# Moving the split weights of a transformer block by 64 bytes in SBUF

## The chip, the core and the metric

The kernel runs as one program on one core of a Trainium2 chip. The metric is the device time of one execution in microseconds (us). Times before: 2294.86 us, the median of three runs (2291.57 to 2296.39).

## What is computed

One transformer block on x, 512 tokens by 2048 features, in float32:

```python
h    = rms_norm(x, norm_mix_pre)
proj = h @ w_in                      # 2048 x 6680: attention q, six k/v sets, gates, retention q, k, v, g
o_a  = nsa_attention(...)            # 8 heads: compressed, selected and window branch, gated
o_r  = silu(g_r) * retention(rope(q_r), rope(k_r), v_r, log_gamma)
x    = x + rms_norm(concatenate([o_a, o_r]) @ w_out, norm_mix_post)
h    = rms_norm(x, norm_mlp_pre)
u    = square(relu(h @ w_up))        # 2048 x 8192
x    = x + rms_norm(u @ w_down, norm_mlp_post)
```

## The kernel before

**Three products for one.** Every large float32 product is made of three matmuls in the type float32r. An operand is split into a high part, which ScalarE makes by casting, and a low part, which VectorE makes by subtracting the high part from the source (`split`, lines 142 to 144; in the feed-forward half lines 948 and 926). `mm3` (lines 153 to 156) then issues high by high, high by low and low by high into one PSUM bank. Of the two operands of a matmul the stationary one (its first) is 128 columns that are loaded into the array by a weight load, the moving one streams past it. Each matmul has a weight load of its own; the names below are in the order moving, stationary, as the profile prints them.

**The operands.** `Hh` and `Hl` hold the split activations (16 slices of 512 columns each). `whi` and `wlo` hold the split weights, in slabs that are fetched from HBM, split and then used. Which is moving and which stationary depends on the stage:

- *Projection w_in.* The first block of it (`v0`) takes its slabs from a pool `early`, 280 columns wide. All others take them from the pool `wp`, slabs of two slices of 512 columns with three buffers. In `feat_major` the activations move (512 columns) and the weights are stationary: `mm<-Hh,whi`. In `tok_major` the weights move (512 columns, in one block 256) and the activations are stationary: `mm<-whi,Hh`. Between these products a second stream of work, the attention and retention units, is issued at fixed points (class `Side`).
- *Output projection w_out.* `tok_major` with the pool `wp`, 416 columns, four blocks; then a last block of 384 columns from a pool `res`.
- *Up projection.* The product with w_up is done by a scheme with seven half-size products per block (`ORDER`), 256 columns of activations moving (`Hh`, `Hl`, or their sums `sx`), the weights stationary: `prod<-Hh,whi`, `prod<-sx,whi`. The slabs come from the pool `hilo` (three buffers of `whi`, three of `wlo`), filled by the class `Feed`, which runs up to three slabs ahead: fetch into `low` or `Y`, sum where the scheme wants one, cast, subtract.
- *Down projection.* The same seven products, with the weights moving (512 columns) and the hidden activations, which now lie in `Hh` and `Hl`, stationary: `prod<-whi,Hh`.

**Where they lie.** A partition of SBUF is one row of bytes. Tile pools on the left side are stacked upward from a fixed start; pools opened with `side="right"` are stacked downward from the top, which in the built program is byte 229344. An unused tile in a pool of its own (`gap_h`, `gap_w`, `gap_r`) therefore only shifts what is stacked after it. On the left `misc` comes first, and `Hh` starts at byte 17056, `Hl` at 49824: both are 160 modulo 256. All their slices are multiples of 512 bytes, so every operand taken from them starts at 160 modulo 256. On the right, in the first half of the kernel, the raw slabs (`wr`, 3 x 4096 bytes) come first, then `gap_w` with 128 bytes, then `wp` (6 x 4096 bytes), which so starts at 192352, or 96 modulo 256; below it lie the tiles of the retention units. In the second half all these have been released, and `hilo` (6 x 4096 bytes) starts at 204768, or 224 modulo 256, with `low` below it. The sums `sx` lie at 160, the slabs of `res` at 64. A slab in `early` has 2240 bytes, which is 192 more than a multiple of 256, so its eight slabs start at four different places.

With the place of the moving operand minus that of the stationary one, modulo 256 and as a signed number, the large products before are:

| products | moving, stationary | columns | matmuls | difference, bytes |
|---|---|---|---|---|
| w_in, `feat_major` | Hh/Hl, whi/wlo in `wp` | 512 | 1536 | +64 |
| w_in, `tok_major` | whi/wlo in `wp`, Hh/Hl | 512 | 768 | -64 |
| w_in, `tok_major` | whi/wlo in `wp`, Hh/Hl | 256 | 192 | -64 |
| w_in, `v0` | whi/wlo in `early`, Hh/Hl | 280 | 192 | eight values |
| w_out | whi/wlo in `wp`, Hh/Hl | 416 | 768 | -64 |
| w_out, last block | whi/wlo in `res`, Hh/Hl | 384 | 192 | -96 |
| up | Hh/Hl/sx, whi/wlo in `hilo` | 256 | 5376 | -64 |
| down | whi/wlo in `hilo`, Hh/Hl | 512 | 2688 | +64 |

The lines that decide this are:

```python
    gw = wctx.enter_context(tc.tile_pool(name="gapw", bufs=1, side="right"))
    gw.tile([P, 32], F32, name="gap_w")
    wp = wctx.enter_context(tc.tile_pool(name="wp", bufs=3, side="right"))
    ...
    hp = ctx.enter_context(tc.tile_pool(name="hilo", bufs=3, side="right", reuse_waits="tile"))
    rw = ctx.enter_context(tc.tile_pool(name="raws", bufs=1, side="right", reuse_waits="tile"))
```

Of the kernel before, what the change touches and what calls it, by code (L numbers as in the profile page):

```python
# [10 lines left out]
F32 = mybir.dt.float32  # L11
# [5 lines left out]
P = 128  # L17
# [95 lines left out]
def block_kernel(ctx: ExitStack, tc: tile.TileContext, x, norm_mix_pre, w_in, cmp_pe_k, cmp_w1_k, cmp_b1_k,  # L113
# [149 lines left out]
    side = Side()  # L263
# [33 lines left out]


    gw = wctx.enter_context(tc.tile_pool(name="gapw", bufs=1, side="right"))
    gw.tile([P, 32], F32, name="gap_w")  # L300
    wp = wctx.enter_context(tc.tile_pool(name="wp", bufs=3, side="right"))
    pool_a = lambda: (wp, S)
    actx, rctx = ExitStack(), ExitStack()
# [560 lines left out]

    ptp = ctx.enter_context(tc.tile_pool(name="ptp", bufs=2, space=PS, side="right"))
    pr0 = ctx.enter_context(tc.tile_pool(name="pr0", bufs=1, space=PS, side="right"))
    hp = ctx.enter_context(tc.tile_pool(name="hilo", bufs=3, side="right", reuse_waits="tile"))
    rw = ctx.enter_context(tc.tile_pool(name="raws", bufs=1, side="right", reuse_waits="tile"))
    low = rw.tile([P, 6144], F32, name="low")
# [518 lines left out]
```

## Time and profile before

| | |
|---|---|
| median of the runs | 2294.86 us |
| the profiled execution | 2292.01 us |
| its span, first to last instruction | 2290.2 us |
| TensorE matmul busy | 2193.3 us (96% of the span), 12787 matmuls |
| weight loads busy | 1923.0 us (84%) |
| VectorE busy | 1563.9 us (68%) |
| ScalarE busy | 986.9 us (43%) |
| mean granted TensorE clock | 0.986 |

A matmul's own duration in the profile includes the time that its first column needs to reach the end of the array, and successive matmuls overlap. So the time that a matmul takes from the engine is read from the start of one to the start of the next, in the view that lists instructions in order of time, or from the number of matmuls in a stretch in which the engine never waits.

### The profile page before, as it was taken

The numbers are of one execution on the slowest core, as the hardware profiler recorded it, in microseconds if no ns is written. First come the engines' busy times: TensorE is split into PE (matmuls) and PEld (weight loads), VectorE is DVE, ScalarE is ACT, GpSimd is POOL, SyncE is SP. The second block draws the span as 40 slices with busy tenths as digits, with TensorE's granted clock in tenths as the row PEclk, the third lists the DMA queues.
The fourth block names the chain that finished last, engine by engine and source line by source line (L and its number), as shares of the span: only waits on it lengthen the run. The fifth ranks groups of instructions, "written<-read, shape, count | busy, mean of one in ns | idle before, by whom it ended". The sixth has DMA issues, their size and how long they took to land.

```text
span 2290.2 us, 31776 instructions
## 1 busy us (share of the span) xinstructions
PE 2193.3 (96%) x12787; PEld 1923.0 (84%) x12787; DVE 1563.9 (68%) x1868; ACT 986.9 (43%) x1432; POOL 122.1 (5%) x133
## 2 busy tenths in 40 slices
PE   8799999999999999989999999999899999999994
PEld 7578878878787899879899999999777888888873
DVE  6122556554655533487788888888768998899897
ACT  5022344243232323464455555555554444444442
POOL 0000000000000000000000000000000000000002
PEclk9899999999999999989999999999999999999997
DMA  6552322322223334557867676767565656566555
GB/s 190 88 154 88 111 69 88 97 74 79 82 82 119 105 105 133 181 177 203 217 193 197 180 196 178 196 179 208 174 227 165 203 160 202 153 200 176 180 151 83
DMA packets 251622, 346.02 MB, mean 151 GB/s; under 512 B 14315, under 2 KB 163131, under 8 KB 250833
## 3 DMA queue, kind: packets, MB, share of 16 engines
q1 hardware_dynamic: 210960, 287.18, 38.9%
q0 software_dynamic: 30416, 45.25, 12.6%
q10 hardware_dynamic: 10098, 11.55, 1.5%
q8 instruction: 100, 1.64, 0.3%
q14 instruction: 48, 0.39, 0.0%
HBM read 299.90 MB, written 44.04 MB: 150 GB/s over the span
## 4 chain that ended last, share of the span: by engine, by line
PE 75%; DVE 11%; DMA 6%; ACT 3%; issue 3%; POOL 1%; SPq 0%; POOLq 0%; ACTq 0%; DVEq 0%
PE prod L155 13%; PE prod L156 13%; PE prod L154 13%; PE mm L154 10%; PE mm L156 10%; PE mm L155 10%; DVE wlo L926 3%; DMA raw<-in_w_in 3%; DMA low<-in_w_up 2%; DVE Hl L144 2%; PE S L580 2%; ACT whi L948 1%; DVE Y L944 1%; DVE low L944 1%; DVE acc L1284 1%
## 5 line engine op out<-in xcount | busy, mean ns | idle before, releaser
L948 ACT CAST whi<-low 128x1024 fp32r<-128x1024 f32 x234 | 245.3, 1052 | 306.4 <-DVE low L944 116.0
L155 PE MATMUL prod<-wlo,Hh 128*128 128x512 f32 x896 | 354.6, 396 | 15.6 <-DVE wlo L926 15.1
L144 DVE TENSOR_TENSOR wlo<-raw,whi 128x1024 fp32r<-128x1024 f32 (+4 forms) x152 | 168.5, 1113 | 283.5 <-ACT whi L143 272.2
L156 PE MATMUL prod<-whi,Hl 128*128 128x512 f32 x896 | 352.2, 393 | 0.0
L154 PE MATMUL prod<-whi,Hh 128*128 128x512 f32 x896 | 350.7, 391 | 0.0
L948 ACT CAST whi<-Y 128x1024 fp32r<-128x1024 f32 x214 | 223.9, 1049 | 287.8 <-DVE Y L944 107.2
L926 DVE TENSOR_TENSOR wlo<-low,whi 128x1024 fp32r<-128x1024 f32 x234 | 285.1, 1222 | 63.1 <-ACT whi L948 61.4
L156 PE MATMUL prod<-Hh,wlo 128*128 128x256 f32 x1024 | 286.6, 280 | 12.7 <-DVE wlo L926 12.7
L926 DVE TENSOR_TENSOR wlo<-Y,whi 128x1024 fp32r<-128x1024 f32 x214 | 260.6, 1222 | 53.6 <-ACT whi L948 52.1
L143 ACT CAST whi<-raw 128x1024 fp32r<-128x1024 f32 (+4 forms) x152 | 145.5, 959 | 333.4 <-PE mm L155 127.3
L154 PE MATMUL prod<-Hh,whi 128*128 128x256 f32 x1024 | 286.3, 280 | 2.9 <-DVE Y L821 2.3
L155 PE MATMUL prod<-Hl,whi 128*128 128x256 f32 x1024 | 285.4, 279 | 0.0
L154 PE MATMUL mm<-whi,Hh 128*128 128x416 f32 (+4 forms) x704 | 263.7, 375 | 0.8 <-ACT Hh L143 0.8
L156 PE MATMUL mm<-whi,Hl 128*128 128x416 f32 (+4 forms) x704 | 249.2, 354 | 0.7 <-DVE Hl L144 0.7
L155 PE MATMUL mm<-wlo,Hh 128*128 128x416 f32 (+4 forms) x704 | 248.9, 354 | 0.0
L154 PE MATMUL mm<-Hh,whi 128*128 128x512 f32 x512 | 218.6, 427 | 15.0 <-ACT whi L143 9.5
L155 PEld LDWEIGHTS prod<-wlo,Hh 128*128 128x128 f32 x896 | 168.5, 188 | 64.8 <-DVE wlo L926 28.1
L156 PE MATMUL prod<-sx,wlo 128*128 128x256 f32 x768 | 214.0, 279 | 6.5 <-DVE wlo L926 6.5
L154 PE MATMUL prod<-sx,whi 128*128 128x256 f32 x768 | 213.7, 278 | 0.8 <-ACT whi L948 0.8
L155 PE MATMUL prod<-sx,whi 128*128 128x256 f32 x768 | 213.5, 278 | 0.0
L156 PEld LDWEIGHTS prod<-Hh,wlo 128*128 128x128 f32 x1024 | 194.5, 190 | 14.5 <-DVE wlo L926 14.4
L156 PE MATMUL mm<-Hh,wlo 128*128 128x512 f32 x512 | 204.2, 399 | 0.1
(259 smaller groups left out, 3953.8 us busy)
## 6 DMA issues: line engine op xcount, KB each, us to landing
raw<-in_w_in SPq DMA_DIRECT2D x160, 256.0 KB, 3.1
low<-in_w_up SPq DMA_DIRECT2D x39, 1024.0 KB, 6.0
Y<-in_w_up SPq DMA_DIRECT2D x33, 1024.0 KB, 6.0
Y<-in_w_down SPq DMA_DIRECT2D x32, 1024.0 KB, 5.3
low<-in_w_down SPq DMA_DIRECT2D x32, 1024.0 KB, 5.2
Y<-ud SPq DMA_DIRECT2D x49, 512.0 KB, 9.0
ud<-Y SPq DMA_DIRECT2D x72, 256.0 KB, 4.7
raw<-in_w_out SPq DMA_DIRECT2D x32, 416.0 KB, 3.4
```

The costliest lines, as they stand in the source:

```text
L143: nc.scalar.copy(hi, src)
L144: nc.vector.tensor_sub(lo, src, hi.bitcast(F32))
L154: nc.tensor.matmul(ps, ah, bh, start=first, stop=False)
L155: nc.tensor.matmul(ps, ah, bl, start=False, stop=False)
L156: nc.tensor.matmul(ps, al, bh, start=False, stop=last)
L580: nc.tensor.matmul(sps[:, :c + L], QT[g][:, h, qs], k, start=True, stop=True)
L926: nc.vector.tensor_sub(lo, src, hi.bitcast(F32))
L944: nc.vector.tensor_add(to, to, by)
L948: nc.scalar.copy(hi, src)
L1284: nc.vector.tensor_add(e[p], ps, e[p])
```

## The change

`gap_w` is made 64 bytes instead of 128, so that everything stacked after it on the right (`wp` and the retention tiles) lies 64 bytes higher: `wp` starts at 192416, or 160 modulo 256. In front of `hilo` a new unused tile of 64 bytes, `gap_m`, is stacked, so that `hilo` and `low` lie 64 bytes lower: `hilo` starts at 204704, or 160 modulo 256. No instruction is added, removed or reordered. The difference of the table becomes 0 in every row except that of `v0` and that of the last block of w_out, which stay as they are.

```diff
     gw = wctx.enter_context(tc.tile_pool(name="gapw", bufs=1, side="right"))
-    gw.tile([P, 32], F32, name="gap_w")
+    gw.tile([P, 16], F32, name="gap_w")
     wp = wctx.enter_context(tc.tile_pool(name="wp", bufs=3, side="right"))
...
     pr0 = ctx.enter_context(tc.tile_pool(name="pr0", bufs=1, space=PS, side="right"))
+    gh = ctx.enter_context(tc.tile_pool(name="gaph", bufs=1, side="right"))
+    gh.tile([P, 16], F32, name="gap_m")
     hp = ctx.enter_context(tc.tile_pool(name="hilo", bufs=3, side="right", reuse_waits="tile"))
```

## Rows read from the trace of the kernel before

**Rows 1.** Busy time by stretch: us, then PE, PEld, DVE, ACT, POOL, PEclk, DMA share, GB/s

```profile
130.00:967.00 837.00, 833.32 (x4181) 709.46 (x4180) 409.39 (x736) 277.55 (x576) 18.06 (x32) 1.00 0.34 100
967.00:1143.00 176.00, 153.32 (x1218) 149.37 (x1218) 138.12 (x147) 93.66 (x123) 12.78 (x11) 0.95 0.71 201
1143.00:1620.00 477.00, 475.69 (x4194) 475.49 (x4195) 387.25 (x388) 266.25 (x327) 30.57 (x24) 1.00 0.68 190
1620.00:2250.00 630.00, 616.08 (x2655) 496.85 (x2655) 556.53 (x484) 302.74 (x313) 37.86 (x32) 1.00 0.60 178
```

**Rows 2.** Waits from 1143 to 1613 us: us in total, times, longest

```profile
ACT whi L948 <- PE prod L155: 136.5, 123, 1.7
...
PEld prod L156 <- DVE wlo L926: 0.7, 1, 0.7
```

**Rows 3.** Matmuls in order of time, w_in `feat_major`: start us, us, what

```profile
559.85 0.40 PE L154 MATMUL mm<-Hh,whi 128*128 128x512 f32 x1
...
578.87 0.39 PE L156 MATMUL mm<-Hh,wlo 128*128 128x512 f32 x1
```

**Rows 4.** Matmuls in order of time, down projection

```profile
1959.66 0.39 PE L155 MATMUL prod<-wlo,Hh 128*128 128x512 f32 x1
...
1979.11 0.39 PE L156 MATMUL prod<-whi,Hl 128*128 128x512 f32 x1
```

**Rows 5.** Matmuls in order of time, w_in `tok_major`, 512 columns

```profile
731.24 0.39 PE L154 MATMUL mm<-whi,Hh 128*128 128x512 f32 x1
...
750.61 0.39 PE L156 MATMUL mm<-whi,Hl 128*128 128x512 f32 x1
```

**Rows 6.** Busy time in stretches of one product: 416, 384, 256, 256 and 512 columns

```profile
812.00:928.00 116.00, 116.00 (x623) 116.00 (x622) 38.78 (x45) 35.02 (x59) 1.61 (x3) 1.00 0.38 114
930.00:950.00 20.00, 20.00 (x117) 20.00 (x117) 7.23 (x15) 6.98 (x16) 1.65 (x3) 1.00 0.69 216
1030.00:1065.00 35.00, 35.00 (x300) 35.00 (x299) 26.93 (x26) 17.53 (x22) 3.90 (x3) 1.00 0.69 174
1145.00:1610.00 465.00, 465.00 (x4105) 465.00 (x4105) 377.96 (x378) 259.21 (x318) 30.57 (x24) 1.00 0.68 189
1878.00:1926.00 48.00, 48.00 (x211) 39.41 (x210) 41.63 (x36) 19.05 (x19) 2.36 (x2) 1.00 0.56 154
```

**Rows 7.** Busy time and granted clock just after a wait, 256 columns

```profile
972.20:975.00 2.80, 2.80 (x15) 2.80 (x15) 1.69 (x2) 2.19 (x3) 0.00 (x0) 0.50 0.00 0
```

**Rows 8.** Matmuls in order of time in that stretch

```profile
973.06 0.41 PE L155 MATMUL prod<-Hl,whi 128*128 128x256 f32 x1
...
974.98 0.41 PE L155 MATMUL prod<-Hl,whi 128*128 128x256 f32 x1
```

**Rows 9.** Matmuls in order of time, `v0`, last two slabs, 280 columns

```profile
47.86 0.29 PE L154 MATMUL mm<-whi,Hh 128*128 128x280 f32 x1
...
48.25 0.29 PE L154 MATMUL mm<-whi,Hh 128*128 128x280 f32 x1
...
48.63 0.29 PE L154 MATMUL mm<-whi,Hh 128*128 128x280 f32 x1
...
49.02 0.29 PE L154 MATMUL mm<-whi,Hh 128*128 128x280 f32 x1
...
49.41 0.39 PE L154 MATMUL mm<-Hh,whi 128*128 128x512 f32 x1
```

**Rows 10.** Costliest groups on the page: casts and subtractions from two sources

```profile
L948 ACT CAST whi<-low 128x1024 fp32r<-128x1024 f32 x234 | 245.3, 1052 | 306.4 <-DVE low L944 116.0
L948 ACT CAST whi<-Y 128x1024 fp32r<-128x1024 f32 x214 | 223.9, 1049 | 287.8 <-DVE Y L944 107.2
L926 DVE TENSOR_TENSOR wlo<-low,whi 128x1024 fp32r<-128x1024 f32 x234 | 285.1, 1222 | 63.1 <-ACT whi L948 61.4
L926 DVE TENSOR_TENSOR wlo<-Y,whi 128x1024 fp32r<-128x1024 f32 x214 | 260.6, 1222 | 53.6 <-ACT whi L948 52.1
```

## The prediction, made before the changed kernel had run

> **What bounds the kernel now.** I read the busy shares first, then busy time by stretch, then the waits, and last the matmuls one by one. TensorE is busy for 96% of the span. By stretch it has almost no idle time once the start is over: 833.3 of 837 us in the projections and the attention, 475.7 of 477 in the up projection, 616.1 of 630 in the down projection; only in the change from the first half to the second (967 to 1143 us) does it lose 23 us, at a mean granted clock of 0.95 [rows 1]. VectorE is busy for 88% of the down projection (556.5 of 630) and less elsewhere. In the up projection TensorE's longest-waited releaser is worth 0.7 us in 470, while ScalarE waits 136.5 us for TensorE to give slab buffers back [rows 2]: the feed is ahead, the matmuls set the pace. So the time is the number of matmuls times the spacing of their starts, and nothing is in front of TensorE to hide a change of that spacing.
>
> **The spacing is larger than the columns ask for, and not everywhere by the same.** The reader divides the time between two rows by the matmuls between them (the count is mine, from the full list of the stretch).
>
> - 512 columns, moving operand 64 bytes above the stationary one (modulo 256): 83 intervals from 559.85 to 578.87 us, 229.2 ns each [rows 3]; in the down projection 85 intervals from 1959.66 to 1979.11, 228.8 ns [rows 4]. I take 229.0.
> - 512 columns, moving operand 64 bytes below: 83 intervals from 731.24 to 750.61, 233.4 ns [rows 5].
> - 416 columns, 64 below: 116 us hold 623 rows, of which two began before or are cut off, so 186.8 ns; 384 columns, 96 below: 20 us for 115, 173.9 ns [rows 6].
> - 256 columns, 64 below: 465 us for 4103 matmuls, 113.3 ns, without a single wait; but from 1030 to 1065 us the same kind of matmul at the same places took 35 us for 298, 117.4 ns [rows 6]. So there are at least two steady rhythms for one placement.
>
> All of these ran at a granted clock of 1.00, the 2.4 GHz level, at which a column takes 0.417 ns: 512 columns 213.3 ns, 416 173.3, 384 160.0, 256 106.7. The surplus is 15.7, 20.1, 13.5, 13.9 and 6.6 (or 10.7) ns. In a stretch with a granted clock of 0.50, the 1.2 GHz level [rows 7], which followed a wait, 9 intervals from 973.06 to 974.98 us give 213.3 ns for 256 columns [rows 8]: exactly the columns, no surplus. So the surplus belongs to the fast clock, when operands are read twice as fast, and between the two placements of 512 columns it differs by 4.4 ns. Roles don't explain that: in rows 4 and 5 alike weights move past `Hh` and `Hl`, and only the places differ.
>
> *What the skill says against it.* The Trainium skill, "TensorE: Matmul & The Clock Gate", Part 2, "Step-by-step: what each phase is for", says that the streaming operand and the weight load have independent read ports in SBUF, so that the next weight load takes no bandwidth from the running matmul; by that rule the place of one against the other changes nothing and the sum is 0. Rows 4 and 5 differ all the same, so the trace does not fully agree; the rule's result is the second rival below.
>
> **The change part by part.** Nothing is added on any queue; three things move.
>
> *The weights in `wp` and `hilo`: the difference becomes 0 in all products but `v0` and the last block of w_out.* The trace of before shows the difference 0 in one place only, the first half of the last slab of `v0`, 280 columns: three matmuls from 48.63 to 49.02 us, 130 ns each. Its neighbours at -64, +32 and +96 bytes took 130, 127 and 130 ns (47.86 to 48.25, to 48.63; 49.02 to 49.41) [rows 9]. That rules out that the surplus goes away at difference 0 (280 columns alone are 116.7 ns), and it shows no penalty, but three matmuls are too few to settle into a rhythm. So I bound 512 columns at difference 0 by the long rows: below by 226.7 ns, which is 213.3 plus the 13.4 that 384 and 416 columns pay, above by the 233.4 of rows 5. Difference 0 lies as far from +64 as from -64, so I take the middle of their rows, 231.2 ns. With 1536 + 2688 = 4224 matmuls now at 229.0 and 768 at 233.4, that is 4224 x 2.2 = +9.3 us and 768 x -2.2 = -1.7 us, together +7.6 us. For 256, 384 and 416 columns there is no second placement in a long row; nearest are their own rows, so I leave 113.3 and 186.8 as they are, with 117.4 as the dear end of 256 (4103 matmuls x 4.1 = +16.8 us) and the bare columns as the cheap end (4103 x -6.6 = -27.1 us, and 768 x -13.5 = -10.4 us for 416).
>
> *Other readers and writers of the moved tiles.* The cast of a slab takes 1052 ns from `low` (224 modulo 256) and 1049 ns from `Y` (32 modulo 256), the subtraction 1222 ns from both [rows 10]. So the place does not matter to ScalarE and VectorE by more than 3 ns in 1050, some 2 us over all slabs, and that lies beside TensorE: cost 0.
>
> *The transfers into `low` and into the raw slabs that borrow buffers of `wp`.* They land 64 bytes lower or higher, at the same place modulo 64. If they took longer, the cover is the feed's lead: ScalarE waits 136.5 us for free buffers [rows 2], against 448 casts in all, so a landing could be late by some 0.3 us each before it reached TensorE. I take 0.
>
> The sum against the profiled execution: 2292.0 + 7.6 = 2299.6 us. Its time lies 2.9 us under the median of the runs, so for the median I say 2302.5 us. All of it passes through, since TensorE does not wait where the matmuls are; were 512 columns cheaper instead, VectorE, busy 41.6 of 48 us in the down projection [rows 6], would follow down to 87% of today's time.
>
> **Rivals.**
>
> 1. *The dearer rhythm everywhere.* At difference 0 both streams begin in the same 256-byte place and hinder one another as in the worst rows seen: 512 columns at 233.4 (4224 x 4.4 = +18.6 us) and 256 at 117.4 (+16.8 us): +35.4, 2330 us. For it: the second rhythm exists already, and an operand that trails by 64 costs more than one that leads. Against it: the row at difference 0 is no dearer than its neighbours [rows 9].
> 2. *No dependence on the difference.* Either nothing changes, or only the place of the moving operand itself counts: at 160 and 224 (rows 3 and 4) it costs 229, at 96 (rows 5) 233.4, and after the change all lie at 160, so -4.4 x 768 = -3.4 us. 2291.5 to 2295 us, no change. For it: rows 9, where eight placements cost the same. Against it: rows 3 to 5 fit a difference as well.
> 3. *The other side: faster, because streams in the same place hinder each other once and then run in step.* Then 512 columns would pay what 384 and 416 pay, 226.7 ns: 4224 x -2.3 = -9.7 and 768 x -6.7 = -5.1 us: 2280 us. It decides from 228.5 ns downward for 512 columns, if 256 columns stay. For it: the surplus of 512 columns varies with the place, and that of 416 is smaller with more than two thirds of its columns. Against it: the 280 columns at difference 0 still pay 13.3 ns.
> 4. *The surplus goes away.* 512 columns at 213.3, 256 at 106.7, 416 at 173.3: 66 + 15 + 37 + 10 = -128 us, 2167 us. Against it: rows 9.
>
> That the change does not do what it says is no rival here: the two tiles shift the stack, and the places follow from sizes.
>
> **How the numbers follow.** The forecast, 512 columns between 229.0 and 233.4 and the rest unchanged, gets 0.30; its own range is 2294 to 2314 us, and 0.05 of the 0.30 lies within 0.2% (4.6 us, about what runs of this kernel can tell from no change). Rival 1 gets 0.18, rival 2 0.25 (0.02 of it faster and 0.01 slower by more than 0.2%), rival 3 0.22 (0.01 within), rival 4 0.05. Slower: 0.25 + 0.18 + 0.01 = 0.44. Same: 0.05 + 0.22 + 0.01 = 0.28. Faster: 0.02 + 0.21 + 0.05 = 0.28. The range from 2275 to 2334 us holds the forecast and rivals 1 to 3 with little beyond their prices; rival 4 and the far ends of the others are left out.
>
> **What would show it.** In the profile of the changed kernel: the spacing of 512-column starts in the same three places (229 to 233 ns: forecast; 226.7 or less: rival 3; 229 in all three: rival 2); the number of 256-column matmuls per stretch of the up projection (113.3 ns: forecast; 117.4 or more: rival 1; towards 106.7: rival 4); 416 columns at 186.8 ns; casts and subtractions at 1050 and 1222 ns. The prediction is wrong in kind if the 256-column spacing moves, for I have set it to stay and it has the most matmuls; it is wrong in its base if idle time of TensorE changes by more than a few microseconds where it now waits for nothing.

## The result, and the profile after

The changed kernel takes 2316.73 us (median of 10 runs, 2314.88 to 2318.20), against 2296.05 us for the kernel before on the same chip (median of 10, 2291.57 to 2312.66): 1.0076 times as long, 95% interval 1.0051 to 1.0100. It is slower, by 20.7 us between the medians. One execution of the kernel before in the experiments below took 3644.9 us, at a mean granted clock of 0.557, and counts in no comparison. The profiled execution took 2316.6 us, 24.6 us more than the profiled one of before.

The stretches of the changed kernel, cut at the same points of the work as [rows 1] (us, then PE, PEld, DVE, ACT, POOL, PEclk, DMA share, GB/s):

```profile
130.00:964.00 834.00, 830.50 (x4178) 710.32 (x4177) 408.33 (x734) 276.50 (x572) 18.02 (x32) 1.00 0.34 100
964.00:1145.00 181.00, 160.29 (x1237) 156.59 (x1236) 142.47 (x151) 96.34 (x128) 12.77 (x11) 0.95 0.71 201
1145.00:1648.00 503.00, 502.13 (x4182) 501.93 (x4182) 384.51 (x385) 265.42 (x324) 30.57 (x24) 1.00 0.64 179
1648.00:2275.00 627.00, 611.78 (x2657) 496.88 (x2656) 556.61 (x484) 302.65 (x313) 37.84 (x32) 1.00 0.60 178
```

The reader is to see where the time went. The up projection, the third row, became longer by 26 us with nearly the same number of matmuls (4182 after 4194) and, as before, hardly any idle time of TensorE. The change from the first half to the second became 5 us longer, the projections and the down projection 3 us shorter each. So the spacing of the matmuls changed, in both directions. The same stretches of one product as in [rows 6], in the changed kernel (416, 384, 256, 256 and 512 columns):

```profile
808.00:926.00 118.00, 118.00 (x628) 117.32 (x627) 39.08 (x46) 35.17 (x59) 1.61 (x3) 1.00 0.38 115
930.00:948.00 18.00, 18.00 (x106) 18.00 (x105) 5.83 (x13) 6.54 (x15) 1.20 (x3) 1.00 0.65 208
1030.00:1062.00 32.00, 32.00 (x269) 32.00 (x268) 23.68 (x24) 14.77 (x19) 3.44 (x3) 1.00 0.66 166
1147.00:1640.00 493.00, 493.00 (x4110) 493.00 (x4109) 378.44 (x379) 259.23 (x317) 30.57 (x24) 1.00 0.64 178
1905.00:1950.00 45.00, 45.00 (x200) 37.27 (x199) 39.02 (x34) 17.93 (x18) 2.36 (x2) 1.00 0.59 163
```

With the two records that belong to the edges taken off, 4108 matmuls of 256 columns in 493 us are 120.0 ns each, against 113.3 [rows 6]; the earlier stretch, 267 in 32 us, has 119.9 against 117.4. The 512-column products are read from starts in order of time, three pairs of first and last row: `feat_major` as [rows 3], 82 intervals, `tok_major` as [rows 5], 82, and the down projection as [rows 4], 87:

```profile
558.92 0.39 PE L154 MATMUL mm<-Hh,whi 128*128 128x512 f32 x1
...
577.50 0.39 PE L155 MATMUL mm<-Hl,whi 128*128 128x512 f32 x1
...
729.23 0.39 PE L154 MATMUL mm<-whi,Hh 128*128 128x512 f32 x1
...
747.81 0.39 PE L155 MATMUL mm<-wlo,Hh 128*128 128x512 f32 x1
...
1981.16 0.40 PE L156 MATMUL prod<-whi,Hl 128*128 128x512 f32 x1
...
2000.90 0.39 PE L156 MATMUL prod<-whi,Hl 128*128 128x512 f32 x1
```

They give 226.6, 226.6 and 226.9 ns, where there were 229.2, 233.4 and 228.8. All three products with both operands in the same place, modulo 256 bytes, run alike, whichever operand moves, and all are cheaper than before.

Casts and subtractions did not change, as on the page of the changed kernel (its line numbers are 2 higher there; before: [rows 10]):

```profile
L950 ACT CAST whi<-low 128x1024 fp32r<-128x1024 f32 x234 | 244.9, 1050 | 321.2 <-PE prod L155 107.8
L928 DVE TENSOR_TENSOR wlo<-low,whi 128x1024 fp32r<-128x1024 f32 x234 | 285.0, 1222 | 71.4 <-ACT whi L950 70.0
```

Summing start to start over all matmuls of a product, waits included, accounts for the difference between the two profiled executions: up projection 675.3 us against 645.6 (+29.7), down projection 636.9 against 640.3 (-3.4), 512 columns of w_in 582.5 against 586.4 (-3.9), its 256 columns 23.8 against 23.0 (+0.8), 416 columns 145.0 against 143.9 (+1.1); together +24.3 of the 24.6 us.

### The profile page after: what moved, and what is told of

Same layout as the page of the kernel before. It is cut to its first block, busy times and chain, and to the rows that moved or that the text cites. A ratio compares the mean times of both kernels' runs of the same rounds, so it can differ in the third digit from the quotient of the medians.

```text
span 2314.8 us, 31776 instructions
## 1 busy us (share of the span) xinstructions
PE 2218.8 (96%) x12787; PEld 1957.2 (85%) x12787; DVE 1564.1 (68%) x1868; ACT 987.7 (43%) x1432; POOL 122.0 (5%) x133
## 4 chain that ended last, share of the span: by engine, by line
PE 76%; DVE 11%; DMA 6%; ACT 3%; issue 3%; POOL 1%; SPq 0%; POOLq 0%; ACTq 0%; DVEq 0%
PE prod L155 14%; PE prod L156 13%; PE prod L154 13%; PE mm L154 10%; PE mm L156 10%; PE mm L155 10%; DVE wlo L928 3%; DMA raw<-in_w_in 3%; DMA low<-in_w_up 2%; DVE Hl L144 2%; PE S L580 2%; ACT whi L950 1%; DVE Y L946 1%; DVE low L946 1%; DVE acc L1286 1%
## 5 line engine op out<-in xcount | busy, mean ns | idle before, releaser
L950 ACT CAST whi<-low 128x1024 fp32r<-128x1024 f32 x234 | 244.9, 1050 | 321.2 <-PE prod L155 107.8
L928 DVE TENSOR_TENSOR wlo<-low,whi 128x1024 fp32r<-128x1024 f32 x234 | 285.0, 1222 | 71.4 <-ACT whi L950 70.0
L156 PE MATMUL prod<-Hh,wlo 128*128 128x256 f32 x1024 | 293.0, 286 | 9.5 <-DVE wlo L928 9.4
L928 DVE TENSOR_TENSOR wlo<-Y,whi 128x1024 fp32r<-128x1024 f32 x214 | 260.6, 1222 | 58.5 <-ACT whi L950 57.1
L154 PE MATMUL prod<-Hh,whi 128*128 128x256 f32 x1024 | 292.9, 286 | 2.3 <-DVE Y L821 2.3
L155 PE MATMUL prod<-Hl,whi 128*128 128x256 f32 x1024 | 291.9, 285 | 0.0
L156 PE MATMUL prod<-sx,wlo 128*128 128x256 f32 x768 | 219.3, 286 | 7.7 <-DVE wlo L928 7.7
L154 PE MATMUL prod<-sx,whi 128*128 128x256 f32 x768 | 218.9, 285 | 0.4 <-ACT whi L950 0.4
L155 PE MATMUL prod<-sx,whi 128*128 128x256 f32 x768 | 218.7, 285 | 0.0
```

What stands on the lines that cost most here:

```text
L154: nc.tensor.matmul(ps, ah, bh, start=first, stop=False)
L155: nc.tensor.matmul(ps, ah, bl, start=False, stop=False)
L156: nc.tensor.matmul(ps, al, bh, start=False, stop=last)
L928: nc.vector.tensor_sub(lo, src, hi.bitcast(F32))
L950: nc.scalar.copy(hi, src)
```

## The experiments

In all of them D is the theory that the spacing depends on the columns and on the difference of the places of the two operands modulo 256 bytes, and on nothing else that the change touched. Spacings are from the full list of starts of the longest unbroken stretch.

**One part alone: the pool `wp`.** `gap_w` is 64 bytes and there is no `gap_m`.

```diff
-    gw.tile([P, 32], F32, name="gap_w")
+    gw.tile([P, 16], F32, name="gap_w")
```

> One part of the change alone: gap_w 64 bytes, no gap_m. The slabs in wp lie at difference 0 to Hh and Hl, those in hilo as before (256 columns at -64, 512 columns of the down projection at +64). Theory D (the spacing of matmul starts is set by the difference, modulo 256, of the places of moving and stationary operand, and by the columns): w_in at 512 columns 226.9 ns in feat_major and tok_major alike (before 229.0 and 233.4), 416 columns 188.3 (before 186.7), up projection 113.3 to 117.7, down 229. Sum 1536 x -2.1 + 768 x -6.5 + 768 x 1.6 + 192 x 6.5 = -5.7 us, a ratio of 0.9975. Rival S (the surplus in the up projection comes from something that both gaps shift together, such as all right-hand tiles): part of the +20.7 us stays, the up projection spaced above 118 ns.

Measured: 2307.27 us against 2295.56, ratio 1.0003 (0.9968 to 1.0037). In w_in the spacings came out as D has them: 226.7 and 226.8 ns at 512 columns, 188.3 at 416. But the median says nothing by itself, since the 12 times stand in two groups, 2287 to 2295 us (5) and 2306 to 2312 us (7). The times of the kernel before do so too in this comparison: 25 from 2290.4 to 2296.8, 9 from 2310.7 to 2314.3 us. The profiled execution of this kernel, 2308.3 us, is from the upper group and shows why. Its two stretches of the up projection, to be laid beside the third and fourth of [rows 6]:

```profile
1030.00:1062.00 32.00, 32.00 (x285) 32.00 (x284) 24.87 (x25) 16.25 (x20) 3.90 (x3) 1.00 0.69 178
1142.00:1629.00 487.00, 487.00 (x4138) 487.00 (x4137) 381.49 (x383) 259.83 (x318) 30.59 (x24) 1.00 0.65 183
```

Here the early stretch runs at 113.1 ns and the long one at 117.7; in the profiled execution of the kernel before it was the other way round. The operands of the up projection lie in the same places in both kernels. So at -64 there are two rhythms, and one of them holds for the whole unbroken run. 4100 x 4.4 ns = 18 us is the distance between the two groups of times. Group against group this kernel has medians of 2290.0 and 2310.7, the kernel before 2294.2 and 2312.5: faster by 2 to 4 us, where D said 5.7. Its profile has the missing part: the sum over `feat_major` fell by only 0.1 us (395.2 after 395.3), not by 3.2. The side work breaks this product into 102 stretches, of which 82 are of 6 or 12 matmuls. Inside these the spacing is 229.9 ns before and 230.1 here, leaving out intervals over 300 ns; only the long stretches reach 226.7.

**The other part alone: `hilo`.** `gap_w` as before, with `gap_m`.

```diff
+    gh = ctx.enter_context(tc.tile_pool(name="gaph", bufs=1, side="right"))
+    gh.tile([P, 16], F32, name="gap_m")
     hp = ctx.enter_context(tc.tile_pool(name="hilo", bufs=3, side="right", reuse_waits="tile"))
```

> The other part alone: gap_m, with gap_w as before. Theory D: up projection 120.0 ns (5376 matmuls), down projection 226.9, w_in as before (229.0, 233.4, 186.7). The change as a whole gave +20.7 us and its part in wp should give -5.7, so +26.4 us, a ratio of 1.0115. Rival S: less than the whole change, the rest being in wp: between 0 and +20.7 us.

Measured: 2319.84 us against 2295.56 (+24.3), ratio 1.0077 (1.0049 to 1.0106), 12 times from 2316.1 to 2322.1 in one group. The up projection, and below it the down projection:

```profile
1150.00:1643.00 493.00, 493.00 (x4110) 493.00 (x4110) 378.52 (x379) 259.10 (x317) 30.57 (x24) 1.00 0.64 178
1830.00:1877.00 47.00, 47.00 (x209) 38.93 (x208) 41.04 (x36) 18.47 (x19) 2.36 (x2) 1.00 0.55 156
```

120.0 ns and 47 us for 207, 227 ns, while w_in stayed at 228.9, 233.3 and 186.7. By the medians this part alone costs 24.3 us, where D said 26.4 and rival S no more than the 20.7 of the whole change. The intervals of the two ratios overlap, so it is the spacings that decide: with `hilo` alone at 0 the up projection runs at 120.0 ns as in the whole change.

**The down projection at 0 and the up projection at -64.** `gap_w` of 64 bytes, no `gap_m`, and the hidden activations start 16 floats further in `Hh` and `Hl`.

```diff
-    ua = [tuple(H[:, c:c + SL] for H in (Hhf, Hlf)) for c in range(0, 7 * SL, SL)]
+    ua = [tuple(H[:, c:c + SL] for H in (Hhf, Hlf)) for c in range(16, 16 + 7 * SL, SL)]
```

> gap_w 64 bytes and no gap_m, as in the first, and the hidden activations of the down projection start 64 bytes further into Hh and Hl, so that the down projection is at difference 0 while the up projection stays at -64. Theory D: up 113.3 to 117.7 ns, down 226.9, w_in 226.9: -5.7 - 2688 x 2.1 = -11.3 us, a ratio of 0.995. Rival A (it is not the difference but the pair of absolute places, 160 with 160): the down projection, now with both at 224, need not be at 226.9 and stays near 229; -5.7 us.

Measured: 2288.35 us against 2295.56, ratio 0.9964 (0.9933 to 0.9996); 9 of 12 times from 2284.3 to 2290.7, three from 2303.6 to 2307.3. It is the only version timed here whose interval lies under 1. Up and down projection:

```profile
1145.00:1611.00 466.00, 466.00 (x4115) 466.00 (x4113) 378.08 (x378) 259.02 (x317) 30.57 (x24) 1.00 0.68 189
...
1797.13 0.39 PE L156 MATMUL prod<-whi,Hl 128*128 128x512 f32 x1
...
1815.97 0.39 PE L155 MATMUL prod<-wlo,Hh 128*128 128x512 f32 x1
```

113.3 ns, and 83 intervals of 227.0 ns with both operands at 224 modulo 256, where the changed kernel has both at 160. So it is not that pair of places. Lower group against lower group it is 6.4 us faster (2287.8 after 2294.2), not 11.3: beside `feat_major`, the down projection gained only 3.4 us of its 5.6 (636.9 us after 640.3, waits included).

**All places moved by 32 bytes, all differences kept.**

```diff
+    keep.tile([P, 8], F32, name="gap_l")
     Hh = keep.tile([P, KT, S], F32R, name="Hh")
...
-    gw.tile([P, 32], F32, name="gap_w")
+    gw.tile([P, 24], F32, name="gap_w")
...
+    gh = ctx.enter_context(tc.tile_pool(name="gaph", bufs=1, side="right"))
+    gh.tile([P, 56], F32, name="gap_m")
```

> All operands moved by 32 bytes modulo 256, on both sides of SBUF, with all differences as before (+64 and -64): Hh, Hl and sx at 192, wp at 128, hilo at 0. Theory D: as before, 229.0, 233.4, 186.7 and 113.3 to 117.7 ns, ratio 1.000 within 0.3%. Rival A (absolute places, or the place within 64 bytes, count): the spacings differ from before; if starts at multiples of 64 spare one step of 16 columns each, 256 columns go to 106.7 ns and the time falls by up to 5376 x 6.6 = 35 us.

Measured: 2290.74 us against 2295.56, ratio 0.9972 (0.9940 to 1.0003). The spacings are those of before: 228.9 to 229.1 in `feat_major`, 233.2 in `tok_major`, 186.7 at 416 columns, 113.3 and in one stretch 117.8 in the up projection, 83 intervals of 228.9 ns in the down projection:

```profile
1081.00:1096.00 15.00, 15.00 (x130) 15.00 (x129) 12.32 (x13) 6.68 (x9) 1.26 (x1) 1.00 0.38 110
1149.00:1614.00 465.00, 465.00 (x4105) 465.00 (x4104) 377.56 (x379) 257.60 (x315) 30.56 (x24) 1.00 0.67 189
...
1800.89 0.39 PE L157 MATMUL prod<-whi,Hl 128*128 128x512 f32 x1
...
1819.89 0.39 PE L156 MATMUL prod<-wlo,Hh 128*128 128x512 f32 x1
```

Absolute places don't count, not even within 64 bytes; rival A falls. The same kernel bears on the modulus. Modulo 512 its differences are not those of before in two products (448 after 192 in the up projection, 64 after 320 in the down projection), and their spacings stayed; modulo 128, the differences 0 and 128 would be one, and the table below has them apart. So 256 is the modulus that fits. (At difference 0 all long rows lie at 256 modulo 512; 0 modulo 512 was not run.)

The times of its lower group lie 4.5 us under those of before (2289.7 after 2294.2). No spacing explains that; it stays open, and the interval holds 1. So the first and the third kernel, timed in the same comparison, may owe a part of their 2 to 4 and 6.4 us to something other than the spacing too.

**Six other differences.** Each of these kernels ran once, profiled: 2330.3, 2324.0, 2324.9, 2320.9, 2328.6 and 2312.0 us in the order below, beside one execution of the kernel before of 2289.2 us. One execution each says little of the time, so only the spacings are read. Only the sizes of the two gaps differ, in floats `gap_w` / `gap_m`: 8/8, 24/24, 0/32 (no `gap_w`), 32/48, 16/40 and 16/56.

> One look, for the spacing at another difference: up projection at -32, down projection at +32; in w_in feat_major at -32 and tok_major at +32. Theory D1 (what counts is how far apart the two places are, in either direction): between difference 0 and 64, so 256 columns between 113.3 and 120.0 ns, 512 columns between 226.8 and 233.3. Theory D2 (steps: the cost belongs to the 64 bytes in which the two lie against one another): exactly the value of 0 or of 64, 120.0 or 113.3 to 117.8.

> One look: up projection at +32, down projection at -32; feat_major at +32, tok_major at -32. Theory D1: as at the opposite sign. Theory D2: the value of 0 or of +64. Rival (direction counts, as between 229.0 and 233.4 ns at +64 and -64): 256 columns at +32 differ from -32.

> One look: up projection at +64, down projection at -64; feat_major at -64, tok_major at +64, the mirror of the kernel before. If only places and columns count, and not the stage or which tensor moves: feat_major 233.3 ns (was 229.0), tok_major 512 columns 229.0 (was 233.4), down 233.3 (was 229.0). 256 columns at +64 are new: if direction counts for them as for 512, they are cheaper than at -64, that is below 113.3, or in the cheap one of the two rhythms only; if not, 113.3 to 117.8.

> One look: up and down projection at a difference of 128, half of 256 bytes, w_in as before. Theory D1: the two are as far apart as they can be, so 256 columns cheapest of all (113.3 or less, towards 106.7) and one rhythm only. Rival (no order in the distance): anywhere between 113 and 120 ns, and 512 columns between 226.8 and 233.4.

> One look: up projection at +96, down projection at -96, w_in at 0 as in the change. The distance D1 has fallen (at 128 the 256 columns cost 118.7 ns, more than at -64), so: Theory D3 (the spacing depends on the difference without order in it, each value with its own steady rhythm): 256 columns somewhere in 113 to 120 ns, 512 columns in 226.8 to 233.4, and w_in again 226.9 at 512 columns. Rival D2 (steps of 64 bytes): 256 columns at +96 as at +64 (117.8) or at 128 (118.7).

> One look: up projection at -96, down projection at +96, w_in at 0 as in the change. Theory D3: 113 to 120 ns at 256 columns. 384 columns at -96 were 173.4 ns, 13.4 over the bare columns, as little as any; if that holds for 256 columns in proportion (8.9 ns), 115.6 ns, cheaper than the dear rhythm at -64. Rival D2: as at -64 (113.3 or 117.8) or at 128 (118.7).

Up projection of each of the six, in this order, one fence for each kernel. Behind it, for all but the third, stand the first and last row of 209 intervals of the down projection (512 columns), at the difference with the opposite sign:

```profile
1155.00:1643.00 488.00, 488.00 (x4127) 488.00 (x4126) 380.27 (x380) 260.37 (x318) 30.58 (x24) 1.00 0.65 182
...
1754.04 0.40 PE L155 MATMUL prod<-wlo,Hh 128*128 128x512 f32 x1
...
1802.81 0.39 PE L154 MATMUL prod<-whi,Hh 128*128 128x512 f32 x1
```

```profile
1158.00:1637.00 479.00, 479.00 (x4108) 479.00 (x4107) 378.59 (x379) 257.89 (x316) 30.60 (x24) 1.00 0.65 183
...
1747.53 0.40 PE L155 MATMUL prod<-wlo,Hh 128*128 128x512 f32 x1
...
1796.30 0.39 PE L154 MATMUL prod<-whi,Hh 128*128 128x512 f32 x1
```

```profile
1156.00:1639.00 483.00, 483.00 (x4103) 483.00 (x4102) 377.70 (x379) 257.46 (x315) 30.56 (x24) 1.00 0.65 182
...
734.75 0.40 PE L154 MATMUL mm<-whi,Hh 128*128 128x512 f32 x1
...
753.77 0.40 PE L156 MATMUL mm<-whi,Hl 128*128 128x512 f32 x1
```

```profile
1146.00:1636.00 490.00, 490.00 (x4131) 490.00 (x4130) 380.83 (x381) 260.58 (x318) 30.57 (x24) 1.00 0.65 182
...
1746.42 0.40 PE L155 MATMUL prod<-wlo,Hh 128*128 128x512 f32 x1
...
1794.99 0.39 PE L154 MATMUL prod<-whi,Hh 128*128 128x512 f32 x1
```

```profile
1148.00:1641.00 493.00, 493.00 (x4110) 493.00 (x4110) 378.62 (x380) 258.82 (x315) 30.58 (x24) 1.00 0.64 178
...
1751.24 0.40 PE L155 MATMUL prod<-wlo,Hh 128*128 128x512 f32 x1
...
1800.21 0.40 PE L154 MATMUL prod<-whi,Hh 128*128 128x512 f32 x1
```

```profile
1142.00:1626.00 484.00, 484.00 (x4127) 484.00 (x4126) 380.33 (x382) 259.21 (x318) 30.57 (x24) 1.00 0.65 183
...
1736.23 0.39 PE L155 MATMUL prod<-wlo,Hh 128*128 128x512 f32 x1
...
1784.99 0.40 PE L154 MATMUL prod<-whi,Hh 128*128 128x512 f32 x1
```

Dividing as above gives the column for 256; the column for 512 is from the pairs and the lists of starts, that for 416 from the lists. The extra pair of the third kernel is `tok_major` at +64, 83 intervals of 229.2 ns: the mirror of [rows 5], with the value of [rows 3].

| moving minus stationary, bytes | 256 columns, ns | 512 columns, ns | 416 columns, ns |
|---|---|---|---|
| 0 | 120.0 | 226.8 | 188.3 (186.7 in short stretches) |
| +32 | 116.7 (117.8 in one stretch) | 233.3 | 186.7 and 193.3 |
| +64 | 117.8 | 229.0 | 188.3 |
| +96 | 120.0 | 233.3 | |
| 128 | 118.7 (120.0 in one stretch) | 232.4 (233.3 in shorter stretches) | |
| -96 | 117.3 | 234.3 | |
| -64 | 113.3 and 117.8 | 233.3 | 186.7 |
| -32 | 118.3 | 233.3 | 190.0 |
| bare columns at 2.4 GHz | 106.7 | 213.3 | 173.3 |

Neither the distance (D1) nor steps of 64 bytes (D2) order this table. Direction counts at 512 columns: +64 and -64 differ by 4.3 ns. At 256 columns direction had +64 cheaper than -64, and it is not: all its stretches ran at the dear value of -64, and 113.3 ns was seen at -64 alone. What is left is D3, a value for each difference without order in it (several share 233.3), the same in `feat_major`, `tok_major`, up and down wherever two of them share a difference. Of the eight, 0 is the best for 512 columns and with +96 the worst for 256. At 256 columns all values but those of 0 and -64 come from one or two executions, so a second rhythm may have been missed.

**A restart in each block.** The kernel of the third experiment, with one small float32 transpose per block of the up projection.

```diff
+            if p == 2:
+                pt = ptp.tile([P, S], F32, name="PT")
+                nc.tensor.transpose(pt[:, :P], ident, ident)
```

> The kernel e3_up64_down0 (up projection at -64, all 512-column products at 0) with one matmul of another kind added in each of the 16 blocks of the up projection: a float32 transpose of the identity, 128 columns, into a PSUM tile that nobody reads. It cuts the unbroken run of some 4100 matmuls into 16. The two rhythms at -64, 113.3 and 117.8 ns, are 18 us apart over that run. Theory K (the rhythm is settled by how the run begins; behind a float32 matmul without a wait, as in the 256-column block of w_in, which ran at 113.4 in every kernel with -64, it is the cheap one): every block at 113.3, no executions near 2306 any more, all at about 2288 + 16 x 0.3 = 2293 us. Rival C (chance at each beginning): blocks of both rhythms in one execution, and times spread between 2293 and 2310 instead of standing in two groups. Rival N (a single other matmul doesn't touch the rhythm): two groups as before, 2293 and 2311.

Measured: 2295.74 us against 2296.65, ratio 0.9982 (0.9958 to 1.0006), 12 times from 2293.1 to 2299.6 in one group, while the kernel before had 12 from 2290.4 to 2297.6 and 5 from 2309.4 to 2312.7 beside it. Four stretches of the profile, the first three each within one block, the last over two:

```profile
1171.00:1209.00 38.00, 38.00 (x325) 38.00 (x324) 29.91 (x31) 20.52 (x26) 2.35 (x2) 1.00 0.62 178
1211.00:1247.00 36.00, 36.00 (x320) 36.00 (x319) 29.21 (x30) 20.20 (x26) 2.02 (x2) 1.00 0.63 186
1249.00:1287.00 38.00, 38.00 (x325) 38.00 (x324) 29.95 (x30) 20.38 (x26) 2.54 (x2) 1.00 0.64 181
1289.00:1363.00 74.00, 74.00 (x655) 74.00 (x655) 60.10 (x60) 41.31 (x51) 4.29 (x4) 1.00 0.65 186
```

117.6, 113.2, 117.6 and 113.3 ns: blocks of both rhythms in one execution, and each keeps its own to its end. K and N fall, and of the three only C fits: the rhythm is settled at the beginning of each run. That it is chance is not shown. What decides it stays open, and nothing tried here makes it the cheap one. The times fill only the lower part of the 2293 to 2310 us that C allowed. The profiled execution, of 2293.1 us, has both rhythms in it, so 2293 was too high a price for a run with the cheap one alone.

## Why the prediction was right, and where its sum was wrong

**The bound was right.** TensorE sets the pace, and its idle time hardly changed: in the up projection 0.9 us of 503 against 1.3 of 477. Nearly all of the change, 24.3 of 24.6 us, lies between the starts of these products, as the first section of the prediction said it would have to.

**The mechanism was right.** It was that TensorE's starts set the time, and that the difference of the two places sets their spacing. The difference of the two places does set the spacing: the products follow it through thirteen kernels, moving the places and not the difference changes no spacing, and swapping +64 and -64 between `feat_major` and `tok_major` swaps their spacings. The second rival falls: the spacing of every product that the change touched moved. By the rule of the Trainium skill ("TensorE: Matmul & The Clock Gate", Part 2, "Step-by-step: what each phase is for") that loading the next weights takes no SBUF read bandwidth from the running matmul, the spacing of 113.3 ns would have stayed. The trace of the changed kernel, with 120.0 ns, does not agree, though no run shows that the weight load is what the matmul waits for.

**The sign of the result was right by the wrong terms.** That the time rose, and that it stayed inside the range, is luck: the term forecast to cost gained, and the term set at nothing cost. The sum had +7.6 us, all from 512 columns, and 0 from 256. Between the profiled executions 512 columns gave -7.3 us (-3.4 down, -3.9 in w_in) and 256 columns +30.5 (+29.7 up, +0.8 in w_in). The median came out inside the range (2316.7 in 2275 to 2334) but beyond the forecast's own (2294 to 2314), and the price of rival 1 for 256 columns, 117.4 ns, was too low as well.

- *"Difference 0 lies as far from +64 as from -64, so I take the middle of their rows."* This step failed: the spacing is no smooth function of the difference. At 0 it is 226.8 ns, below both neighbours and at the low bound that I had set, which was rival 3's price. A value between two measured ones would have had to be measured.
- *"For 256, 384 and 416 columns there is no second placement in a long row; ... so I leave 113.3 and 186.8 as they are."* This is the term that decided. It had the most matmuls, 5376, and its two rhythms at one placement showed already that 256 columns react to small things. It measured 120.0 ns, above the dear end of 117.4 that I had taken from the other rhythm. The prediction named a moving 256-column spacing as what would make it wrong in kind, and by that test its sum was.
- The 280-column rows at difference 0 [rows 9], which showed no penalty, were no evidence for 256 columns: the table has 0 as the best place for 512 columns and the worst for 256. And three matmuls are no rhythm, as `feat_major` shows, whose broken stretches gained almost nothing. Rival 2 also counted eight placements in these rows; they hold four, at 127 to 130 ns.

**The two edits taken as 0 were 0.** Casts took 1050 ns and subtractions 1222, as before. ScalarE waits even longer for free buffers, 174.4 us in the up projection where it was 136.5 [rows 2], as it must with slower matmuls:

```profile
ACT whi L950 <- PE prod L155: 174.4, 134, 2.1
```

**The base was not one number.** The profiled execution of before had the dear rhythm until 1143 us and the cheap one after it. Executions of before stand in two groups some 18 us apart, those of the changed kernel in one. In the comparison of the result, eight executions of before lie in the lower group, with a median of 2295.3 us, and two at 2311.8 and 2312.7. Against the lower group the change costs some 21 us, against the median of all ten 20.7, and between the two profiles 24.6, since the profiled one of before took 2292.0.

## What to carry to other kernels

Where TensorE sets the pace, place the two operands of the costliest product by measurement, for each width of the moving operand by itself: a shift of 64 bytes was worth 6.7 ns of 113 at one width and had the opposite sign at another. Do not read a spacing off its neighbours, and let a product run some dozens of matmuls unbroken before its spacing is believed: stretches of 6 and 12 showed none of the gain that stretches of 80 and more had. If a kernel's times stand in two groups, compare the spacing of its longest unbroken run between executions before comparing medians.

## What the runs showed of the hardware

- The time of a float32r matmul above its bare columns depends on the difference, modulo 256 bytes, of the places from which its two operands are read: 6.7 to 13.3 ns at 256 columns, 13.5 to 21 at 512. It is gone at the 1.2 GHz level, where 256 columns took 213.3 ns at -64 [rows 7, 8], and in the changed kernel at 0 as well (21 intervals at a granted clock of 0.50, last fence). That two reads of SBUF hinder one another at the fast clock would fit this; which of them waits, and why 0 is good for 512 columns and bad for 256, no run here shows.
- One placement can have two steady rhythms: 113.3 and 117.8 ns for 256 columns at -64, kept for up to 4100 matmuls, and settled anew at each interruption, one float32 transpose being enough. Two were also seen at +32 (116.7 and 117.8) and at 128 (118.7 and 120.0). At 0 only 120.0 ns was seen in the up projection, and the 22 timed executions of the two kernels that have it there stand in one group each; at +96, too, only 120.0 ns was seen, in one execution.

The stretch at the 1.2 GHz level in the changed kernel, its busy time and granted clock, and the first and last row of the 21 intervals:

```profile
970.30:974.90 4.60, 4.60 (x23) 4.60 (x23) 3.45 (x7) 3.23 (x4) 0.04 (x1) 0.50 0.00 0
...
970.29 0.41 PE L155 MATMUL prod<-Hl,whi 128*128 128x256 f32 x1
...
974.77 0.39 PE L155 MATMUL prod<-Hl,whi 128*128 128x256 f32 x1
```
